# Layer 1 of a two-layer attention kernel: the first query products stand ahead of the last key transposes, the key stores get three buffers at another place, and one weight piece is split sooner

## The chip, the cores and the metric

The kernel runs on one core of a Trainium2 chip. The metric is the time of one execution on the device, in microseconds: 1680.79 us before the change, the median of three runs (1679.54 to 1683.7). A core has five engines that each work off a queue of their own in order and wait for one another through semaphores: TensorE (PE, with its weight loads as PEld), VectorE (DVE), ScalarE (ACT), GpSimd (POOL) and SyncE (SP), which here issues nearly all DMAs.

## The reference

Two layers work on 1024 latent tokens and 256 context tokens of width 1024. Each layer normalizes the rows, scales and shifts them by values computed from a condition vector, and runs an attention mixer whose output is gated, projected and added to the input. Layer 0 is grouped-query attention. Layer 1, where the change lies, is multi-head latent attention:

```
kv_a, k_r, q_a, g = split(h @ w_in, [256, 288, 672])
kv     = rms_norm(kv_a, kv_a_norm) @ w_kv_b          # per head: 64 key and 64 value columns
k_nope = rms_norm(kv[..., :64], k_nope_norm)
k_rope = rope(rms_norm(k_r, k_rope_norm))            # one 32-wide key for all heads
q      = rms_norm(rms_norm(q_a, q_a_norm) @ w_q_b, q_norm)   # 16 heads of 96, the last 32 rotated
p      = softmax((q_nope k_nope + q_rope k_rope) / sqrt(96))  # latent queries, all 1280 keys
y      = (p v * silu(g)) @ w_out
```

Context tokens give keys and values in layer 1, but no queries and no output. All data are 32-bit floats.

## The kernel before

**Precision.** Each product of two fp32 matrices is made of three passes on rounded parts, `hi x hi`, `hi x lo` and `lo x hi` (`mm3`, L90). So each operand is split into a high part, a rounded copy made by ACT, and a low part, the difference, made by DVE or POOL. `load_weight` (L139) does it for weights: a piece of up to 1024 columns is fetched by an SP DMA into one of three raw buffers `wraw`, then `parts` casts it on ACT (L158) and subtracts on DVE or POOL (L137, chosen by a counter and the argument `share`; with `share=1` always DVE). With `todo` given, the pieces are not fetched at once but collected as functions: calling a piece issues its DMA and returns a function that splits it. The split weights lie in a ring of two pairs of buffers.

**Stages of layer 1.** Tokens go in ten tiles of 128, eight latent and two context.

1. `out_proj` of layer 0 makes the new rows; `sink0` normalizes them, and `modulate` turns them to columns and splits them. For the last tile, a context tile, it calls `last0` (L1491), which loads the first weight of layer 1 (`l1_w_in`, columns 0 to 287), adds the last output, multiplies tiles 0 and 1 by that weight (`proj1`, kept in `early`), modulates the context (`flush(1)`), and loads and splits `l1_w_kv_b` (256 x 2048, four pieces).
2. The keys: `staged` (L100) runs stages over the tiles, one tile behind the other. `kv_compress` projects and normalizes (`kvn`, L1529), `kv_latent` transposes and splits the latent, `kv_expand` makes keys (`mmk`) and values (`mmv`) by `l1_w_kv_b`, normalizes the keys (`kn`, L1561) and stores the values, and `kv_store` (L1591) transposes the keys on TensorE (L1597), splits them into `th` (ACT, L1601) and `tl` (DVE, L1602), and stores these with two SP DMAs.
3. The queries: `q_compress` (L1714) multiplies by columns 288 to 671 of `l1_w_in` (`wqa`), squares and sums on ACT (L1718), takes the reciprocal root on POOL (`qa_rs`), scales on DVE (`qan`); `q_latent` transposes and splits that; `q_expand` and `q_store` follow. A second pass makes the other heads. The gate's products are mixed in.
4. Attention over 16 heads, then the output projection.

**Order of the work.** Instructions are placed on the engines' queues by a planner that simulates the program by its own costs: on each engine it takes, among those that are ready, the one that comes first in the program. Inside `tc.manual_schedule(engines=...)`, and `in_order(engine)`, the named engines keep the written order of that block; others may still be put in between. Before the change only DVE is kept in order in the key stage, and nothing in the query stage.

**Memory.** Buffers are taken from pools. The pools of one stage lie on a stack (`side="right"`), and the pools of the next stage lie in the same memory; with `reuse_waits="tile"` a new tile waits for the readers and writers of those old tiles that it overlaps, the DMAs that store them among them. In the key stage the stack holds `wk1b` (six working tiles), `stg1a` (two buffers each of `th`, `tl` and the values `v1`), `latp1a` (four of each latent part) and small tiles. In the query stage `wk1c` (eight working tiles, `sq` and `qan` among them), `stg1b`, `latp1b`, `wqp` (a split weight) and small tiles lie there. Product results lie in PSUM: four buffers `mm` and four `tp` for transposes.

Of the kernel before, what the change touches and what calls it, by code (L numbers as in the profile page):

```python
# [11 lines left out]
F32R = mybir.dt.float32r  # L12
# [7 lines left out]
P = 128  # L20
D = 1024
KT = D // P
# [4 lines left out]
TT = NT // P  # L27
# [5 lines left out]
def raw(ap):  # L33
    return ap.bitcast(F32)
# [3 lines left out]
def hybrid_kernel(ctx: ExitStack, tc: tile.TileContext, ins: dict, out: bass.AP):  # L38
# [12 lines left out]
    def pad(pool, size):  # L51

        pool.tile([P, size // 4], F32, name="pad", tag="pad", bufs=1)
# [28 lines left out]
    def in_order(engine):  # L82

        return tc.manual_schedule(engines={engine})
# [15 lines left out]
    def staged(items, *stages):  # L100

        items = list(items)
        held = {}
        for t in range(len(items) + len(stages) - 1):
            for j, stage in enumerate(stages):
                i = t - j
                if 0 <= i < len(items):
                    held[i] = stage(items[i], held.get(i))
# [17 lines left out]
    def ring_pair(dtype=F32R):  # L126
        a = ring.tile([P, 4096], dtype, name="wa", tag="wa")
        b = ring.tile([P, 4096], dtype, name="wb", tag="wb")
        return a, b
# [3 lines left out]
    def sub_any(lo, a, b, share):  # L133

        lo_turn[0] += 1
        eng = dve if share and lo_turn[0] % share == 0 else pool
        eng.tensor_sub(lo, a, b)  # L137

    def load_weight(w, kt, c0, cols, share=2, slot=None, todo=None):  # L139
        a, b = slot or ring_pair()  # L140
        pitch = -(-cols // 64) * 64
        wh, wl = (t[:, : kt * pitch].rearrange("p (k n) -> p k n", n=pitch)[:, :, :cols] for t in (a, b))
        src = w[:, c0:c0 + cols].rearrange("(k p) n -> p k n", p=P)
        wid = min(cols, 1024)
        step = max(1, 1024 // cols)
        for k in range(0, kt, step):
            for c in range(0, cols, wid):
                n = min(step, kt - k)

                def piece(k=k, n=n, c=c):  # L150
                    r = rawp.tile([P, 1024], F32, name="wraw", tag="wraw")
                    rv = r[:, : n * wid].rearrange("p (k n) -> p k n", n=wid)
                    ks, cs = slice(k, k + n), slice(c, c + wid)
                    sp.dma_start(rv, src[:, ks, cs])

                    def parts(share=share):
                        for j in range(n):
                            act.copy(wh[:, k + j, cs], rv[:, j, :])  # L158
                            sub_any(wl[:, k + j, cs], rv[:, j, :], raw(wh[:, k + j, cs]), share)

                    return parts

                if todo is None:
                    piece()()
                else:
                    todo.append(piece)
        return wh, wl
# [114 lines left out]
    def h_cols(hT, tt):  # L282

        hh, hl = hT[0 if tt < TL else 1]
        cs = slice((tt % TL) * P, (tt % TL + 1) * P)
        return (lambda k: hh[:, k, cs]), (lambda k: hl[:, k, cs])
# [572 lines left out]
    right = dict(side="right", reuse_waits="tile")  # L859
# [7 lines left out]
    small = stR.enter_context(tc.tile_pool(name="sml0", bufs=3, **right))  # L867
    wk = stR.enter_context(tc.tile_pool(name="wk0", bufs=6, **right))
    tab = stR.enter_context(tc.tile_pool(name="tab0", bufs=1, **right))
    sg2 = []  # L870
# [262 lines left out]
    parts = [[ModPart(0, sec, q, 256, lambda: mp[0], 4, wk, ps_mod, ps_tp) for q in range(4)] for sec in range(2)]  # L1133
# [279 lines left out]
    w_in1 = ins["l1_w_in"]  # L1413
    hT1 = []

    def proj1(tt, w, cols):
        ps = ps_mm.tile([P, 512], F32, name="mm", tag="mm")
        lh, ll = h_cols(hT1, tt)
        mm3(ps[:, :cols], lh, ll, lambda k: w[0][:, k, :], lambda k: w[1][:, k, :], range(KT))
        return ps  # L1420
# [32 lines left out]
    with ExitStack() as st:  # L1453
        xp = st.enter_context(tc.tile_pool(name="xpp0", bufs=4, **right))
        gp = st.enter_context(tc.tile_pool(name="gp0", bufs=1, **right))
        wk = st.enter_context(tc.tile_pool(name="wk1a", bufs=3, **right))
        small = st.enter_context(tc.tile_pool(name="sml1a", bufs=3, **right))
        pad(small, 224)
        stO = ExitStack()
        op = stO.enter_context(tc.tile_pool(name="opp0", bufs=3, **right))  # L1460
        hold = []

        def flush(upto):
            while len(hold) >= upto and hold:
                pair, xs = hold.pop(0)
                modulate(1, pair, xs, hT1, ps_tp, wk)

        xs_of = {}

        def sink0(tt, xt):  # L1470
            if tt < TL:
                sp.dma_start(x1d[tt * P:(tt + 1) * P, :], xt)
            norm_rows(xt, small)
            xs_of.setdefault(tt // 2, []).append(xt)
            if tt % 2 == 0:
                flush(1)
            else:
                hold.append((tt // 2, xs_of[tt // 2]))

        def started0():  # L1480
            at.flush()
            stL.close()
            hT1.append(alloc_hT(stl, "hlat1", NL))

        def resid0(tt):
            return x_in[tt * P:(tt + 1) * P, :] if tt < TL else ctx_in[(tt - TL) * P:(tt - TL + 1) * P, :]

        kv_w = []
        early = {}

        def last0(add):  # L1491
            kv_w.append(load_weight(ins["l1_w_in"], KT, 0, 288))
            with tc.manual_schedule(engines={mybir.EngineType.PE, mybir.EngineType.DVE, mybir.EngineType.Activation}):
                add()
                for tt in range(2):
                    early[tt] = proj1(tt, kv_w[0], 288)
                stO.close()
                hT1.append(alloc_hT(stc, "hctx1", NC))
                flush(1)
                kv_w.append(load_weight(ins["l1_w_kv_b"], 2, 0, 2048, 1))  # L1500

        out_proj(0, wo, resid0, sink0, TT, op, xp, gp, ps_mm, first, started0, False, last0)
    hT = hT1

# [2 lines left out]

    with ExitStack() as st:
        wk = st.enter_context(tc.tile_pool(name="wk1b", bufs=6, **right))
        sg2 = st.enter_context(tc.tile_pool(name="stg1a", bufs=2, **right))  # L1510
        latp = st.enter_context(tc.tile_pool(name="latp1a", bufs=4, **right))
        small = st.enter_context(tc.tile_pool(name="sml1b", bufs=3, **right))

        wkvr, wkvb = kv_w
# [76 lines left out]
        def kv_store(tt, held):  # L1591
            cs = slice(tt * P, (tt + 1) * P)
            for g2 in range(2):
                kn = held[g2]
                tp = ps_tp.tile([P, 512], F32, name="tp", tag="tp")
                for j in range(4):
                    pe.transpose(tp[:, j * P:(j + 1) * P], kn[:, j * P:(j + 1) * P], ident)  # L1597
                th = sg2.tile([P, 4, P], F32R, name="th", tag="th")
                tl = sg2.tile([P, 4, P], F32R, name="tl", tag="tl")
                tv = tp.rearrange("p (a n) -> p a n", n=P)  # L1600
                act.activation(th, tv, AF.Copy, scale=w_kn)  # L1601
                dve.scalar_tensor_tensor(tl, tv, w_kn, raw(th), op0=ALU.mult, op1=ALU.subtract)  # L1602
                sp.dma_start(k1h[4 * g2:4 * g2 + 4, :, cs].rearrange("a p n -> p a n"), raw(th))
                sp.dma_start(k1l[4 * g2:4 * g2 + 4, :, cs].rearrange("a p n -> p a n"), raw(tl))

        with in_order(mybir.EngineType.DVE):
            staged(range(TT), kv_compress, kv_latent, later, later, kv_expand, kv_store)
    stK.close()
    stc.close()

# [82 lines left out]
    with ExitStack() as st:  # L1693
        wk = st.enter_context(tc.tile_pool(name="wk1c", bufs=8, **right))
        sg2 = st.enter_context(tc.tile_pool(name="stg1b", bufs=2, **right))
        latp = st.enter_context(tc.tile_pool(name="latp1b", bufs=3, **right))
        wqp = st.enter_context(tc.tile_pool(name="wqp", bufs=1, **right))
        small = st.enter_context(tc.tile_pool(name="sml1c", bufs=3, **right))

        tab = st.enter_context(tc.tile_pool(name="tab1c", bufs=1, **right))  # L1700
        cwq = tab.tile([P, TL, 96], F32, name="cwq")
# [7 lines left out]
                pool.tensor_mul(swq[:, :, o_:o_ + 8], sinB[:, :, o_:o_ + 8],  # L1709
                                w_q[:, 64 + i_:64 + i_ + 8].unsqueeze(1).broadcast_to([P, TL, 8]))  # L1710

        wqa = load_weight(w_in1, KT, 288, 384)

        def q_compress(tt, _):  # L1714
            ps = proj1(tt, wqa, 384)
            ss = small.tile([P, 1], F32, name="qass", tag="qass")
            sq = wk.tile([P, 512], F32, name="sq", tag="w512")
            act.activation(sq[:, :384], ps[:, :384], AF.Square, accum_out=ss)  # L1718
            rs = rstd_of(small, ss, 384, "qa")
            qn = wk.tile([P, 512], F32, name="qan", tag="w512")  # L1720
            dve.scalar_tensor_tensor(qn[:, :384], ps[:, :384], rs, w_qa, op0=ALU.mult, op1=ALU.mult)
            return qn
# [169 lines left out]
```

## Time and profile before

| | |
|---|---|
| median of three runs | 1680.79 us |
| the profiled execution, its own time | 1686.67 us |
| its span, first to last instruction | 1684.9 us |
| mean granted TensorE clock | 0.996 |
| TensorE busy | 1648.9 us |
| VectorE, ScalarE, GpSimd busy | 1046.5, 640.7, 950.6 us |

The profile gives for each engine the busy time in any stretch of the span, and for each instruction its start, its length and what ended the idle time before it. The granted clock is the share of full speed at which TensorE ran. Layer 1's projections begin near 855 us, its key stage fills 855 to 967 us, and the query stage follows up to about 1115 us. Times below are microseconds from the span's start.

### The profile page before, as it was taken

How to read it: one execution, taken by the hardware profiler on the slowest of the kernel's cores; microseconds unless marked ns; L12 is line 12 of the kernel's file. 1: busy time of each engine (PE TensorE's matmuls, PEld its weight loads, DVE VectorE, ACT ScalarE, POOL GpSimd, SP SyncE). 2: the span in 40 equal slices, each digit the busy share in tenths (PEclk: the TensorE clock that was granted, in tenths of full speed). 3: DMA queues.
4: the chain of work that ended last, by engine and by line, in shares of the span. 5: the costliest groups of instructions: out<-in, count | busy, mean ns of one | idle time of the engine just before them, and what ended most of it. 6: DMA issues, size and time to landing. Idle time of an engine off the chain costs nothing. (4 is left out here: it accounts for less than half of the span.)

```text
span 1684.9 us, 27275 instructions
## 1 busy us (share of the span) xinstructions
PE 1648.9 (98%) x10236; PEld 1194.2 (71%) x10236; DVE 1046.5 (62%) x1660; ACT 640.7 (38%) x944; POOL 950.6 (56%) x624
## 2 busy tenths in 40 slices
PE   7999999999999999999989999999999999999998
PEld 5776768875555555468878798886766767767587
DVE  3774553457788877526575657744777777677231
ACT  3642222225454554433244633330534434334310
POOL 2673441118899898833245645450668778777521
PEclk9999999999999999999999999999999999999999
DMA  8548856532352422256324857776566555653451
GB/s 290 194 126 254 253 163 197 156 91 58 83 138 77 126 74 72 79 156 186 125 81 137 241 166 195 222 207 150 127 139 141 133 131 120 133 134 81 121 172 70
DMA packets 221116, 244.21 MB, mean 145 GB/s; under 512 B 23160, under 2 KB 160616, under 8 KB 220984
## 3 DMA queue, kind: packets, MB, share of 16 engines
q1 hardware_dynamic: 220560, 242.36, 51.7%
q8 instruction: 81, 1.33, 0.4%
q14 instruction: 51, 0.42, 0.1%
q10 hardware_dynamic: 424, 0.11, 0.0%
HBM read 168.62 MB, written 73.63 MB: 144 GB/s over the span
## 5 line engine op out<-in xcount | busy, mean ns | idle before, releaser
L552 ACT ACTIVATE p<-st 128x1024 f32<-128x1024 f32 x328 | 335.9, 1027 | 156.9 <-PE st L545 143.2
L586 POOL TENSOR_TENSOR acp<-acp,p 128x1024 f32<-128x1024 f32 x128 | 305.2, 2384 | 8.3 <-ACT p L552 0.4
L394 DVE TENSOR_REDUCE m<-mx 128x1 f32<-128x512 f32 x256 | 176.2, 691 | 94.0 <-PE mx L392 88.1
L430 DVE TENSOR_REDUCE m<-mx 128x1 f32<-128x1024 f32 x128 | 150.4, 1220 | 68.9 <-PE mx L421 68.4
L586 POOL TENSOR_TENSOR acp<-p 128x1024 f32<-128x1024 f32 x34 | 81.5, 2399 | 185.5 <-ACT p L552 185.3
L602 PE MATMUL avt<-p,v 128*64 128x512 f32 x672 | 152.6, 598 | 0.6 <-DVE crow L461 0.3
L586 POOL TENSOR_TENSOR acp<-acp,acd 128x1024 f32<-128x1024 f32 x60 | 142.0, 2366 | 14.6 <-DVE acd L572 11.2
L572 DVE TENSOR_REDUCE acd<-p 128x512 f32<-128x1024 f32 x124 | 144.7, 1220 | 6.9 <-ACT p L552 6.9
L602 PE MATMUL av<-p,v 128*64 128x512 f32 x640 | 141.1, 595 | 0.0
L137 POOL TENSOR_TENSOR wb<-wraw,wa 128x512 fp32r<-128x512 f32 (+3 forms) x65 | 88.4, 1374 | 82.2 <-ACT wa L158 82.2
L94 PE MATMUL mm<-wa,hh 128*128 128x512 f32 (+2 forms) x336 | 127.6, 380 | 1.1 <-ACT hh L959 1.1
L96 PE MATMUL mm<-wa,hl 128*128 128x512 f32 (+2 forms) x336 | 122.0, 363 | 1.5 <-DVE hl L962 1.5
L545 PE MATMUL st<-QH,KH 64*128 64x512 f32 x320 | 122.2, 407 | 0.6 <-DVE gth L304 0.5
L95 PE MATMUL mm<-wb,hh 128*128 128x512 f32 (+2 forms) x336 | 121.3, 361 | 0.0
L545 PE MATMUL st<-QH,KL 64*128 64x512 f32 x320 | 117.7, 391 | 0.0
L545 PE MATMUL st<-QL,KH 64*128 64x512 f32 x320 | 117.2, 390 | 0.0
L94 PE MATMUL y<-wa,oh 128*128 128x512 f32 (+1 forms) x296 | 114.1, 385 | 0.6 <-ACT oh L798 0.6
L95 PE MATMUL y<-wb,oh 128*128 128x512 f32 (+1 forms) x296 | 113.5, 384 | 0.0
L96 PE MATMUL y<-wa,ol 128*128 128x512 f32 (+1 forms) x296 | 113.5, 384 | 0.0
L602 PEld LDWEIGHTS av<-p,v 128*64 128x64 f32 x640 | 44.4, 137 | 88.3 <-issue 87.6
L602 PEld LDWEIGHTS avt<-p,v 128*64 128x64 f32 x672 | 44.9, 136 | 86.9 <-issue 80.6
L94 PE MATMUL mm<-hh,wa 128*128 128x512 f32 (+1 forms) x264 | 103.2, 391 | 0.1
(247 smaller groups left out, 4039.2 us busy)
## 6 DMA issues: line engine op xcount, KB each, us to landing
mraw<-in_l_w_mod SPq DMA_DIRECT2D x64, 256.0 KB
wraw<-in_l_w_in SPq DMA_DIRECT2D x28, 512.0 KB
KH<-k1h SPq DMA_DIRECT2D x32, 320.0 KB
KL<-k1l SPq DMA_DIRECT2D x32, 320.0 KB
rb<-rrow SPq DMA_DIRECT2D x72, 128.0 KB
mraw<-in_l_w_mod SPq DMA_DIRECT2D x16, 512.0 KB
QA<-q0h SPq DMA_DIRECT2D x32, 256.0 KB
wraw<-in_l_w_out SPq DMA_DIRECT2D x16, 512.0 KB
```

The costliest lines, as they stand in the source:

```text
L94: pe.matmul(ps, lhsT=lh(k), rhs=rh(k), start=first and i == 0, stop=False)
L95: pe.matmul(ps, lhsT=lh(k), rhs=rl(k), start=False, stop=False)
L96: pe.matmul(ps, lhsT=ll(k), rhs=rh(k), start=False, stop=last and i == len(ks) - 1)
L137: eng.tensor_sub(lo, a, b)
L394: dve.reduce_max(s["m"][:, i, n:n + 1], held["m"], axis=AX.X)
L430: dve.reduce_max(s["m"][:, i, 0:1], m, axis=AX.X)
L545: pe.matmul(ps[:, n * 512:(n + 1) * 512], lhsT=lh, rhs=rh, start=j == 0, stop=j == last)
L552: act.activation(p, ps, AF.Exp, scale=self.ops["scale"])
L572: dve.reduce_sum(t[:, ns], p2.rearrange("p a n -> p n a")[:, ns, :], axis=AX.X)
L586: pool.tensor_add(t, a, b)
L602: pe.matmul(s["av"][64 * n:64 * n + 64, :], lhsT=s["v"][:, kt, u["vc"]:u["vc"] + 64], rhs=p[:, n * 512:(n + 1) * 512], start=kt == kts[0], ...
```

## The change

- In `last0`, `l1_w_kv_b` is taken in pieces: the DMAs of the first three are called ahead of `add()`; the first piece is split, and the fourth fetched, right behind the two early products and ahead of the context modulation; the other three pieces are split where all four were.
- `kv_store` of the last tile is taken out of the key stage. `wqa` is loaded directly behind that stage, and a block with written order on PE and DVE holds the first query tile's 24 products, then the last tile's `kv_store`. `q_compress` takes the first tile's result from `early`.
- `th` and `tl` have three buffers. The pool of the latents, `latp1a`, lies ahead of `stg1a` on the stack, and in the query stage the small tiles lie ahead of `wqp`.

```diff
         def last0(add):
             kv_w.append(load_weight(ins["l1_w_in"], KT, 0, 288))
             with tc.manual_schedule(engines={mybir.EngineType.PE, mybir.EngineType.DVE, mybir.EngineType.Activation}):
+                todo = []
+                kv_w.append(load_weight(ins["l1_w_kv_b"], 2, 0, 2048, 1, todo=todo))
+                parts = [piece() for piece in todo[:3]]
                 add()
                 for tt in range(2):
                     early[tt] = proj1(tt, kv_w[0], 288)
+                parts[0]()
+                parts.append(todo[3]())
                 stO.close()
                 hT1.append(alloc_hT(stc, "hctx1", NC))
                 flush(1)
-                kv_w.append(load_weight(ins["l1_w_kv_b"], 2, 0, 2048, 1))
+                for part in parts[1:]:
+                    part()
...
         wk = st.enter_context(tc.tile_pool(name="wk1b", bufs=6, **right))
+        latp = st.enter_context(tc.tile_pool(name="latp1a", bufs=4, **right))
         sg2 = st.enter_context(tc.tile_pool(name="stg1a", bufs=2, **right))
-        latp = st.enter_context(tc.tile_pool(name="latp1a", bufs=4, **right))
...
-                th = sg2.tile([P, 4, P], F32R, name="th", tag="th")
-                tl = sg2.tile([P, 4, P], F32R, name="tl", tag="tl")
+                th = sg2.tile([P, 4, P], F32R, name="th", tag="th", bufs=3)
+                tl = sg2.tile([P, 4, P], F32R, name="tl", tag="tl", bufs=3)
...
+        kept = []
+
+        def store_all_but_last(tt, held):
+            kept.append(held) if tt == TT - 1 else kv_store(tt, held)
+
         with in_order(mybir.EngineType.DVE):
-            staged(range(TT), kv_compress, kv_latent, later, later, kv_expand, kv_store)
+            staged(range(TT), kv_compress, kv_latent, later, later, kv_expand, store_all_but_last)
+        wqa = load_weight(w_in1, KT, 288, 384)
+        with tc.manual_schedule(engines={mybir.EngineType.PE, mybir.EngineType.DVE}):
+            early[0] = proj1(0, wqa, 384)
+            kv_store(TT - 1, kept[0])
...
+        small = st.enter_context(tc.tile_pool(name="sml1c", bufs=3, **right))
         wqp = st.enter_context(tc.tile_pool(name="wqp", bufs=1, **right))
-        small = st.enter_context(tc.tile_pool(name="sml1c", bufs=3, **right))
...
-        wqa = load_weight(w_in1, KT, 288, 384)
-
         def q_compress(tt, _):
-            ps = proj1(tt, wqa, 384)
+            ps = early.pop(tt, None) or proj1(tt, wqa, 384)
```

## The prediction

> **What bounds the kernel now.** I read the page first, then the busy time by stretches, then TensorE's instructions in order of time with their waits, and last the chain of waits.
>
> ```profile
> span 1684.9 us, 27275 instructions
> PE 1648.9 (98%) x10236; PEld 1194.2 (71%) x10236; DVE 1046.5 (62%) x1660; ACT 640.7 (38%) x944; POOL 950.6 (56%) x624
> ```
>
> TensorE is busy for all but 36.0 of 1684.9 us, so the change can only earn what TensorE idles, or runs slowly, in the two places that it touches. The stretches show these places (columns: stretch; busy of PE, weight loads, DVE, ACT, POOL; granted clock; DMA share; GB/s):
>
> ```profile
> 860.00:890.00 30.00, 25.42 (x154) 22.14 (x153) 19.80 (x55) 13.24 (x40) 11.21 (x21) 0.89 0.30 95
> ...
> 960.00:990.00 30.00, 25.15 (x140) 23.83 (x140) 15.74 (x27) 14.64 (x30) 15.78 (x12) 0.94 0.86 258
> 990.00:1010.00 20.00, 20.00 (x119) 19.93 (x118) 13.44 (x41) 4.85 (x12) 8.40 (x13) 1.00 0.24 71
> ...
> 880.00:885.00 5.00, 5.00 (x15) 3.71 (x16) 2.08 (x10) 1.99 (x9) 2.75 (x10) 0.50 0.23 77
> 980.00:985.00 5.00, 4.58 (x20) 4.51 (x21) 3.40 (x7) 4.14 (x10) 4.02 (x3) 0.66 0.54 165
> ```
>
> Idle are 30 - 25.42 = 4.6 us at the start of the layer 1 keys and 30 - 25.15 = 4.9 us where keys hand over to queries. Behind them none is idle in 20: a microsecond won at either place is passed on. At both the clock falls (0.50, 0.66), behind these waits (columns: start, length, engine, line, operation, and in brackets the idle time before it and its releaser):
>
> ```profile
> 876.59 0.40 PE L96 MATMUL mmk<-wa,kvl 128*128 128x512 f32 x1
> 879.96 0.66 PE L1548 MATMUL tp<-ident,kvn 128*128 128x128 f32 x2 [2.97 <-DVE kvn L1529]
> 880.27 0.78 PE L94 MATMUL mmv<-wa,kvh 128*128 128x512 f32 x1
> ...
> 886.15 0.39 PE L94 MATMUL mmv<-wa,kvh 128*128 128x512 f32 x1
> ...
> 887.51 0.29 PE L94 MATMUL mm<-wa,hh 128*128 128x288 f32 x1
> ...
> 962.34 1.03 PE L1597 MATMUL tp<-ident,kn 128*128 128x128 f32 x8
> 965.34 0.63 PE L1597 MATMUL tp<-ident,kn 128*128 128x128 f32 x4 [1.97 <-DVE kn L1561]
> ...
> 966.94 0.63 PE L1597 MATMUL tp<-ident,kn 128*128 128x128 f32 x4 [0.80 <-DVE kn L1561]
> 967.33 0.42 PE L95 MATMUL mm<-wb,hh 128*128 128x384 f32 x1
> ...
> 978.01 0.34 PE L96 MATMUL mm<-wa,hl 128*128 128x384 f32 x1
> 980.42 0.52 PE L1728 MATMUL tp<-ident,qan 128*128 128x128 f32 x3 [2.08 <-DVE qa_ms L118]
> ...
> 981.30 0.41 PE L94 MATMUL mm<-wa,hh 128*128 128x384 f32 x1
> ...
> 984.72 0.39 PE L94 MATMUL mm<-wa,hh 128*128 128x384 f32 x1
> ```
>
> The slow clock has a price beside the idle time. Between 880.27 and 886.15 stand 12 key and value products and 4 small transposes in 5.88 us; the six products from 886.15 to 887.51 took 1.36, so at full clock this were 2.72 + about 0.35 = 3.1: 2.8 us lost. Between 967.33 and 978.01 are 61 query products at 0.175 us; from 981.30 to 984.72 nine products and three transposes took 3.42, at full clock 1.58 + 0.27: 1.6 us lost. So the first place holds 2.97 + 2.8 = 5.8 us, the second 1.97 + 0.80 + 2.08 + 1.6 = 6.4 us.
>
> **Part one, the expansion weight.** Its four pieces pass through three raw buffers, so the fourth is fetched only when the first has been split:
>
> ```profile
> 854.98 17.32 SPq L154 DMA_DIRECT2D wraw<-in_l_w_kv_b  x4
> ...
> 875.90 1.05 ACT L158 CAST wa<-wraw 128x1024 fp32r<-128x1024 f32 x1 [3.07 <-DMA wraw<-in_l_w_kv_b]
> ...
> 861.85 1.90 DVE L275 TENSOR_SCALAR hmod<-tp,A,B 128x256 f32<-128x256 f32 x4 [1.28 <-PE tp L271]
> ...
> 870.72 3.49 DVE L137 TENSOR_TENSOR wb<-wraw,wa 128x1024 fp32r<-128x1024 f32 x3
> ...
> 875.31 0.42 DVE L88 TENSOR_TENSOR kvl<-tp,kvh 128x256 fp32r<-128x256 f32 x1
> 876.99 1.22 DVE L137 TENSOR_TENSOR wb<-wraw,wa 128x1024 fp32r<-128x1024 f32 x1 [1.26 <-ACT wa L158]
> 878.13 0.27 DVE L88 TENSOR_TENSOR krl<-tp,krh 32x128 fp32r<-32x128 f32 x1
> 879.33 0.48 DVE L1529 SCALAR_TENSOR_TENSOR kvn<-mm,kvrs,bc_l_kv_a_norm 128x256 f32<-128x256 f32 x1 [0.81 <-POOL kvrs L1527]
> 879.89 0.42 DVE L88 TENSOR_TENSOR kvl<-tp,kvh 128x256 fp32r<-128x256 f32 x1
> 880.62 0.28 DVE L88 TENSOR_TENSOR krl<-tp,krh 32x128 fp32r<-32x128 f32 x1 [0.32 <-ACT krh L87]
> ...
> 881.84 0.48 DVE L1529 SCALAR_TENSOR_TENSOR kvn<-mm,kvrs,bc_l_kv_a_norm 128x256 f32<-128x256 f32 x1 [0.82 <-POOL kvrs L1527]
> ```
>
> VectorE's queue holds the subtraction for the fourth piece ahead of `krl` and of the third tile's `kvn`, for which TensorE waits 2.97 us. After the change one cast (1.05 us or a little less) and one subtraction (1.22) move ahead of the context modulation. VectorE has a hole of 1.28 us ahead of its first `hmod`, into which 1.22 fits; without that cover the modulation slips by at most 1.22, and TensorE has products to do then. The fourth DMA leaves near 862, not 872.3 (854.98 + 17.32), and has landed long before the three remaining pieces are split, in the 3.49 us where three are split now. SP is set free as early; the three other DMAs that move pass no store, as the last output tile is a context tile. The four context low parts swap engines (the counter that alternates DVE and POOL is one further); that I cost at nothing, plus or minus 0.7 us, half a piece's subtraction.
>
> Then `krl` follows `kvl` as it does one tile later, 880.62 - 879.89 = 0.73: at 876.04 in place of 878.13. All behind it is 2.09 us earlier: `kvn` at 877.24, the transposes at 877.87, a wait of 0.9 us behind 876.99. What is late next is the same chain for the fourth tile: from `kvn` to `kvn` it takes 881.84 - 879.33 = 2.51 us, against about 1.7 us of full-clock work, so another 0.8 us, and its small rope part perhaps 0.5. Started at 877.87, with 18 products (880.27 to 887.51) in 3 x 1.36 = 4.1 us, transposes in about 0.6 and these 1.3, the next tile's projection starts near 883.9 instead of 887.51: 3.6 us. I take 3.0, as the planner sets TensorE's order here and won't place each transpose where it fits. Ends: 2.1, if the clock falls nevertheless, and 5.8, if no wait is left.
>
> **Part two, the first query products ahead of the last transposes.** The weight for them was split long before:
>
> ```profile
> 942.49 0.55 DVE L137 TENSOR_TENSOR wb<-wraw,wa 128x384 fp32r<-128x384 f32 x1
> ...
> 960.49 0.59 ACT L1583 COPY v<-mmv 128x512 f32<-128x512 f32 x1 [0.26 <-DMA vd<-v]
> ...
> 964.50 0.69 DVE L1561 TENSOR_TENSOR kn<-mmk,kn_rs 128x512 f32<-128x512 f32 x1 [1.02 <-POOL kn_rs L120]
> ```
>
> So 24 products of 0.175 = 4.2 us stand from 963.1 to 967.3, and the last eight transposes follow at 967.3; their inputs are there at 965.2 and 966.8. Both waits are covered: 2.8 us won. The lower end: the products need one of four PSUM buffers. One comes free with the value copy at 961.1, the next key buffer only at 965.2; were it that one, 2.1 us of the 2.8 would be lost: 0.7.
>
> **Part three, three key buffers and other places.** The query wait of 2.08 us hangs on this piece of the chain:
>
> ```profile
> 967.94 4.23 DMA k1h<-th
> 972.27 0.70 ACT th L1601
> ...
> 973.77 4.20 DMA k1l<-tl
> 978.23 0.59 ACT sq L1718 x2
> 979.07 0.56 POOL qa_rs L120
> ```
>
> The last `th` waits for a store to leave its buffer, and the first `sq` waits for the store of the last `tl`, although it reads nothing of it: the new tile lies where the old one was. With three buffers the first wait goes; with the latents moved between, `sq` lies on latents, whose products ended by 962.3. Behind the products' end at 967.3 `sq` to transposes takes 980.42 - 978.23 = 2.2 us, so about 969.8, if POOL is free. It isn't:
>
> ```profile
> 967.02 4.35 POOL L137 TENSOR_TENSOR wqb<-wraw,wqa 128x768 fp32r<-128x768 f32 x2 [0.94 <-ACT wqa L158]
> ```
>
> If both these splits stay ahead of `qa_rs`, it starts at 971.4 and the transposes at 971.4 + (980.42 - 979.07) = 972.7. TensorE has its transposes to 968.1 and the second tile's products to 972.3. I expect a wait of 0.6 us: of 2.08 + 1.6 = 3.7 the change keeps 3.0, say 2.7 for the new ties (the query latents now lie on the last `th` and `tl`, and ACT's next `sq` is queued behind the one that waits for those stores). Ends: 3.7, and -2.5, if the planner sets the transposes right behind 968.1 (4.6 us and a slow stretch of 1.6).
>
> **The sum.** 3.0 + 2.8 + 2.7 = 8.5 us. The profiled execution took 1686.7 us with a span of 1684.9, the runs' median is 1680.8; idle time and slow clock are absolute, so I take 8.5 from both: 1678.2 profiled, 1672.3 for the median.
>
> The Trainium skill (TensorE: Matmul & The Clock Gate, Part 1) says that the clock halves after at least one idle window of some 3.4 us. Here 2.08 us of idle were enough, with 0.66 granted in the stretch behind, so the measurement decides; taken at its word the rule would say that the gaps are not the cause.
>
> **The rivals.**
> - *The waits move.* TensorE's next inputs come late in both places, and the clock still falls. For it: the fourth tile's chain of 2.51 us and POOL's 4.35 us. Against it: the new waits, 0.9 and 0.6 us, are shorter than 1.97, behind which the products ran on at 0.175. Then 2.1 + 2.8 and a third place at nought: 4.9 at best, with a longer query wait some 3.5; 1677.
> - *The first products don't start early,* for want of a PSUM buffer: 8.5 - 2.1 = 6.4; 1674.4. For it: only one product stood between the two halves of the last transposes. Against it: the copy at 960.49.
> - *The clock falls for a reason other than the gaps.* The slow stretches stay: 2.1 us is left of the 3.0 at the first place, and 2.7 - 1.6 = 1.1 at the third part, with 2.8 between them 6.0; 1674.8. Against it: both stretches directly follow the longest waits.
> - *Slower.* Outside hand-written blocks the planner orders TensorE by its own times. Without the long wait at the start it may set each query tile's transposes too close behind its products, for all eight tiles. The chain from `sq` on is 2.2 us; it decides once fewer than 2.2 / 0.175 = 13 products lie between. At 1.6 us for each tile that is 13 us: 1672.3 + 13 = 1685. Against it: none of the seven later tiles waits now (990 to 1010 is full).
>
> **How the numbers follow.** Forecast 0.58, waits move 0.20, no early start 0.09, clock of its own 0.05, slower 0.08. What a measurement of this kernel tells from no change is about 0.3%, 5.0 us: from 1675.8 to 1685.8. The forecast's own range is 1669 to 1676. Faster: 0.56 of the forecast, 0.06 of no early start, 0.03 of the clock case: 0.65. Slower 0.05, as half of its case lies beyond 1685.8; the rest, 0.30, is within. The range goes from 1667.5 (all 5.8 + 6.4 = 12.2 us won is 1668.6, and the runs lie up to 1.2 below their median) to 1680.5, which leaves out the slower case and little else.
>
> **What would show it.** Right: no DMA wait of ACT at the fourth weight piece, a wait below 1.2 us at the third tile's transposes with clock 1.00 behind it, 24 products of 384 columns straight behind 962 and no `kn` wait, `sq` without a `k1l` wait, clock 1.00 behind the first query transposes. Wrong: a query wait of 2 us on POOL or a store, a clock of 0.5 in either place, or new waits at later query transposes.

## Result: a gain half as large as forecast

The median of 8 runs is 1677.1 us after the change (1676.46 to 1682.35), against 1683.08 of 8 runs of the kernel before beside it. The ratio is 0.9975 (0.9964 to 0.9986), so about 4.2 us are won. It leaves out one run of before that took 1823.73 us, far longer than all others; the medians of the remaining runs lie 5.7 us apart. The same file timed again on another occasion gave 1676.32 against 1681.11, ratio 0.9968 (0.9957 to 0.9979), 5.4 us. Forecast were 8.5 us.

The profiled execution has a span of 1674.9 us, 10 less than the one of before. That difference flatters the change, since the profiled execution of before, at 1686.7 us, was one of its longest. Of the 10 us, 3.0 had arisen before layer 1 began, where nothing was changed. The stretches of the changed kernel (columns as in the prediction):

```profile
860.00:890.00 30.00, 25.03 (x152) 20.90 (x152) 18.79 (x58) 14.12 (x47) 13.09 (x25) 1.00 0.25 78
960.00:990.00 30.00, 30.00 (x182) 29.83 (x181) 19.81 (x39) 13.92 (x31) 17.72 (x16) 1.00 0.84 247
...
1010.00:1030.00 20.00, 18.22 (x106) 16.91 (x105) 16.19 (x46) 7.95 (x18) 10.46 (x13) 1.00 0.77 222
```

At the start of the keys TensorE still idles 5.0 us of 30. At the handover it idles not at all, and its clock is 1.00 in both. So the second place went as planned and the first did not. TensorE's rows at the two places (start, length, engine, line, operation, and in brackets the idle time and its releaser):

```profile
858.19 1.91 PE L271 MATMUL tp<-ident,xt 128*128 128x128 f32 x16
...
865.37 0.44 PE L1554 MATMUL tp<-ident,kvn 128*128 128x128 f32 x2 [1.31 <-DVE kvn L1535]
...
870.17 0.41 PE L1554 MATMUL tp<-ident,kvn 128*128 128x128 f32 x2 [1.22 <-DVE kvn L1535]
...
873.74 0.47 PE L94 MATMUL mmk<-wa,kvh 128*128 128x512 f32 x1 [0.65 <-DVE kvn L1536]
...
876.98 0.41 PE L1554 MATMUL tp<-ident,kvn 128*128 128x128 f32 x2 [1.19 <-DVE kvn L1535]
...
957.79 1.03 PE L1603 MATMUL tp<-ident,kn 128*128 128x128 f32 x8
962.85 1.03 PE L1603 MATMUL tp<-ident,kn 128*128 128x128 f32 x8
972.74 0.49 PE L1741 MATMUL tp<-ident,qan 128*128 128x128 f32 x3
```

In the lower half all waits of 1.97, 0.80 and 2.08 us are gone. In the upper half the wait of 2.97 us for the third tile's `kvn` became one of 1.19, but these transposes still stand 876.98 - 858.19 = 18.8 us behind the last context transposes. Before, it was 879.96 - 861.21 = 18.75. These are the rows of before ahead of the third tile:

```profile
861.21 1.91 PE L271 MATMUL tp<-ident,xt 128*128 128x128 f32 x16
...
866.16 0.44 PE L1548 MATMUL tp<-ident,kvn 128*128 128x128 f32 x2 [1.19 <-DVE kvn L1529]
...
870.14 0.28 PE L1549 MATMUL tp<-ident,kvn 128*32 128x128 f32 x1 [0.38 <-DVE kvn L1541]
```

Up to there TensorE waited 1.19 + 0.38 = 1.6 us before and 1.31 + 1.22 + 0.65 = 3.2 after. So what was won at the third tile (2.97 - 1.19 = 1.8) had been lost at the first two.

### The profile page after: what moved, and what is told of

It is laid out like the page before. It is cut to its first block, busy times and chain, and to the rows that moved or that the text cites. A ratio compares the mean times of both kernels' runs of the same rounds, so it can differ in the third digit from the quotient of the medians.

```text
span 1674.9 us, 27270 instructions
## 1 busy us (share of the span) xinstructions
PE 1643.2 (98%) x10236; PEld 1189.1 (71%) x10236; DVE 1046.0 (62%) x1660; ACT 640.3 (38%) x944; POOL 949.0 (57%) x624
## 3 DMA queue, kind: packets, MB, share of 16 engines
q8 instruction: 81, 1.33, 0.3%
## 4 chain that ended last, share of the span: by engine, by line
PE 83%; DVE 6%; POOL 4%; issue 3%; DMA 2%; ACT 1%; SPq 0%; ACTq 0%; DVEq 0%; POOLq 0%
PE st L545 19%; PE avt L602 8%; PE av L602 8%; PE mm L94 7%; PE mm L96 7%; PE mm L95 7%; PE mx L392 4%; PE y L94 3%; PE y L95 3%; PE y L96 3%; PE mx L421 2%; PE mx L647 1%; PE pm L201 1%; DVE wb L137 1%; PE mx L402 1%
```

## Experiments

A gain is the ratio's distance from 1 times the median of before in the same comparison (1681.1 to 1682.2 us); the medians' own differences lie within 1.1 us of it.

**The changed kernel again, the two halves apart, and the engines' turns.** The first run is the changed file, unaltered. The next two each make one half of the change: only the weight piece in `last0`, or only the handover with its buffers and places. The fourth is the whole change with the context low parts on the engines that they had before:

```
                 parts[0]()
+                lo_turn[0] -= 1
                 parts.append(todo[3]())
                 ...
                 flush(1)
+                lo_turn[0] += 1
```

> The changed kernel as it is, to see how executions spread. Between the two profiled executions the span fell by 9.95 us, of which 3.0 us were won before layer 1 began, where nothing was changed. Theory 1 (the waits and their slow clock are always there): the change is worth about 7 us in every pair, ratio 0.9958. Theory 2 (the slow clock behind a wait comes in some executions only): 4 to 5 us on the mean, ratio 0.997 to 0.9975, and executions with a lower mean clock are the longer ones, by half of the time at half clock.

> Only the weight piece is split sooner; keys and queries as before. The forecast's sum says 3.0 us of gain at the first place (16.4 us from the context's transposes to the third tile's, in place of 18.75). The theory from the traces: 18.8 us as in the changed kernel, since the third tile's transposes are held by the same queue on VectorE, and about 1.5 us to the next projection if the clock stays full; timed 0 to 2 us.

> Only the handover is changed; the weight piece as before. Forecast: 5.5 us at the second place. From the traces: 6.9 us between the eighth tile's key transposes and the fourth query tile's, where slow clock had 1.6 of it, and some 1.4 us given back in the second query pass; timed 4 to 5.5 us. If instead the gain hangs on both parts together, this kernel alone gains less than 3.

> The changed kernel, with the counter that alternates DVE and POOL taken one back ahead of the context modulation and put right behind it, so that the four context low parts are on the engines that they had before the change. Theory: in the changed kernel the fourth low part sits on POOL ahead of the second tile's reciprocal root (867.55 to 868.85), VectorE waits 1.81 us for it with three weight subtractions queued behind, and this eats the 2.09 us that the early piece should win. Then here the third tile's transposes follow the context's first ones after 16.5 to 17 us in place of 18.8, and the span is 1.5 to 2.1 us shorter than the changed kernel's. Rival: the chain of the tiles on VectorE sets the pace whatever the engines; then 18.8 stays.

Measured: the changed kernel again 1676.32. The weight piece alone 1680.82, ratio 0.9999 (0.999 to 1.0008): nothing. The handover alone 1677.19, 0.9974 (0.9966 to 0.9983): 4.4 us, all of the gain. The whole with the old turns 1675.3, 0.9963 (0.9951 to 0.9976): 6.2 us. The 0.9968 of the changed kernel lies between the two theories about the slow clock (0.9958 and 0.997) and decides neither. The halves came out as expected from the traces. With the old turns the third tile's transposes stand 16.92 us behind the context's, as expected, but the time is only 1.0 us below the changed kernel's, not 1.5 to 2.1; and the step that counts turned out to be another than the second tile's reciprocal root, as the next rows show.

**The weight piece with the old turns.** The same two lines in the kernel that has only the first half.

> Part one alone, but the four context low parts stay on the engines that they had before. Theory: the swap of engines, costed at nothing in the forecast, made the first tile's latent transposes 2.23 us later and ate what part one won; without it they stand 4.9 us behind the last context transposes (7.18 with the swap), the third tile's near 16.5 us (18.75 before), and the time is 1.9 us below that of part one with the swap, about 1679. Rival: the place had little to win, since the 6.8 us of half clock in the profile of before are not in most runs; then the transposes come sooner, and the time is still within 1 us of the kernel before (1681).

Measured: 1678.75, ratio 0.9986 (0.9977 to 0.9995), a gain of 2.35 us where the same half without the two lines had none. That is the theory's figure, not the rival's. GpSimd's queue shows why; first the changed kernel, then this one with TensorE's rows:

```profile
862.85 1.29 POOL L137 TENSOR_TENSOR hl<-hmod,hh 128x512 fp32r<-128x512 f32 x1 [6.08 <-ACT hh L279]
864.09 0.70 POOL L1533 TENSOR_TENSOR kvrs<-kvms,mhalf 128x2 f32<-128x2 f32 x1
```

```profile
859.26 1.29 POOL L137 TENSOR_TENSOR hl<-hmod,hh 128x512 fp32r<-128x512 f32 x1 [3.78 <-ACT hh L279]
860.51 0.71 POOL L1535 TENSOR_TENSOR kvrs<-kvms,mhalf 128x2 f32<-128x2 f32 x1
```

```profile
856.90 1.91 PE L271 MATMUL tp<-ident,xt 128*128 128x128 f32 x16
...
861.79 0.44 PE L1556 MATMUL tp<-ident,kvn 128*128 128x128 f32 x2 [1.13 <-DVE kvn L1537]
...
873.86 0.41 PE L1556 MATMUL tp<-ident,kvn 128*128 128x128 f32 x2 [1.23 <-DVE kvn L1537]
```

GpSimd holds the first tile's `kvrs` behind its first context part. With the old turns that is the part that is ready first, 859.26 - 856.90 = 2.36 us behind the context transposes. With the turns swapped it is the next one, 862.85 - 858.19 = 4.66 us behind. So `kvrs`, `kvn` and the first transposes come 2.3 us later (7.18 us behind the context transposes in place of 4.89). VectorE, which keeps the written order, carries the delay on to the third tile. First the changed kernel, then the one with the old turns:

```profile
864.83 0.48 DVE L1535 SCALAR_TENSOR_TENSOR kvn<-mm,kvrs,bc_l_kv_a_norm 128x256 f32<-128x256 f32 x1 [1.70 <-POOL kvrs L1533]
...
869.94 3.49 DVE L137 TENSOR_TENSOR wb<-wraw,wa 128x1024 fp32r<-128x1024 f32 x3
```

```profile
861.25 0.48 DVE L1537 SCALAR_TENSOR_TENSOR kvn<-mm,kvrs,bc_l_kv_a_norm 128x256 f32<-128x256 f32 x1 [1.33 <-POOL kvrs L1535]
...
866.36 3.49 DVE L137 TENSOR_TENSOR wb<-wraw,wa 128x1024 fp32r<-128x1024 f32 x3
```

From the first `kvn` to the three splits it takes 5.11 us in both, so nothing more is lost between them. The pairs of kernels differ by about as much: the halves alone by 2.2 us (2.35 and 0.17), the whole by 1.0 us of time, and by 1.9 us in the trace up to the first key transposes (33.8 and 31.9 us from the last context transposes).

**A second profile of before.**

> The kernel before once more, for a second profile of it. The forecast took the slow clock of both places (2.8 and 1.6 us) as part of every execution. If so, the granted clock is about 0.5 again behind the 2.97 us wait for the third tile's normalised keys and about 0.66 behind the 2.08 us query wait, and from the last context transposes to the ninth tile's key transposes it takes 101 us as in the first profile. Rival: the waits come each time but the slow clock only in some executions; then the waits of 2.97, 1.97, 0.80 and 2.08 us are all there, and a stretch whose clock stayed at 1.00 is shorter by 1.7 us for each 3.4 us of half clock that is missing: 97.7 to 99.4 us.

It took 1681.59 us (span 1679.8). The waits came again (those for the last keys with 1.82 and 0.80 us), the query wait shorter, and half as much half clock came at the first place, none at the second:

```profile
877.79 0.53 PE L1548 MATMUL tp<-ident,kvn 128*128 128x128 f32 x2 [3.02 <-DVE kvn L1529]
...
976.91 0.52 PE L1728 MATMUL tp<-ident,qan 128*128 128x128 f32 x3 [1.31 <-DVE qa_ms L118]
```

```profile
870.00:890.00 20.00, 16.95 (x91) 13.97 (x90) 11.96 (x37) 8.35 (x31) 8.45 (x19) 0.91 0.38 118
...
970.00:990.00 20.00, 18.69 (x112) 18.32 (x111) 11.35 (x27) 8.90 (x22) 10.27 (x11) 1.00 0.88 260
```

From the last context transposes to the ninth tile's key transposes it took 100.75 us, 0.38 less than in the first profile, although 3.4 us less of it ran at half clock; 1.7 us was the rival's figure. The theory that the slow clock belongs to every execution falls, and the rival's price of it is too high as well.

**Each half of the handover alone.** One kernel has only the early products, with two key buffers and the pools where they were. The other has only three buffers and the new places. A third is the whole change, with the old turns, and two key buffers:

```
-                th = sg2.tile([P, 4, P], F32R, name="th", tag="th", bufs=3)
-                tl = sg2.tile([P, 4, P], F32R, name="tl", tag="tl", bufs=3)
+                th = sg2.tile([P, 4, P], F32R, name="th", tag="th")
+                tl = sg2.tile([P, 4, P], F32R, name="tl", tag="tl")
```

> Only the first query tile's 24 products stand ahead of the last eight key transposes; key stores in two buffers and all pools where they were. If parts two and three add up as in the forecast, the waits of 1.97 and 0.80 us for the normalised keys are gone, the query wait of about 2 us stays, and the time falls by 2.8 us (1678.3). Rival: the two need each other, the wait is only moved on to the query transposes, which still hang on the stores of the last keys; then the time falls by less than 1 us.

> Only the three key buffers and the pools' new places; the first query tile's products stand behind the last transposes, as before. If parts two and three add up as in the forecast, the query wait (2.08, 1.31 us in two profiles of before) shrinks to 0.6 or less, the 1.97 and 0.80 us for the normalised keys stay, and the time falls by 2.7 us (1678.6). Rival: with the last stores out of the way the wait was the price of the order alone, and the parts are one thing, of which this half is worth 4 us or more, since the first half alone made the kernel slower.

> The changed kernel with the low parts' engines as before, but the key parts in two buffers again; pools in their new places. If the third buffer is needed, the last key parts on ScalarE wait for a store (2.7 us in the kernel with early products alone), the first query squares are queued behind them, and TensorE waits 1 to 3 us for the first query transposes: 1677 to 1679. If the places alone do it, the squares wait for no store and the time stays at 1675.

Measured: early products alone 1686.08, ratio 1.0035 (1.0023 to 1.0047), slower by some 5.9 us. Places and buffers alone 1681.41, 0.9993 (0.9984 to 1.0002), no difference. Two buffers 1679.07, 0.9987 (0.9977 to 0.9997), so 4 us of the 6.2 are lost without the third buffer. Of these expectations the additive ones failed for both halves: +5.9 and -1.2 do not add to -4.4. The early products' rival had the wait rightly moved on to the query transposes, but had not expected a loss. For places alone the rival's 4 us or more failed too. For two buffers the expectation held, though the wait came out longer than its 1 to 3 us. In the kernel with early products alone, TensorE's and ScalarE's rows, and the stretch behind the wait, are:

```profile
979.97 0.87 PE L1735 MATMUL tp<-ident,qan 128*128 128x128 f32 x3 [5.22 <-DVE qa_ms L118]
```

```profile
969.39 0.69 ACT L1601 ACTIVATE th<-tp,w_kn 128x512 fp32r<-128x512 f32 x1 [2.68 <-DMA k1h<-th]
...
977.77 0.49 ACT L1725 ACTIVATE sq<-mm 128x384 f32<-128x384 f32 x1 [2.00 <-DMA k1l<-tl]
```

```profile
980.00:985.00 5.00, 5.00 (x21) 4.90 (x22) 3.77 (x6) 2.46 (x7) 3.58 (x4) 0.60 0.45 121
```

The query chain is tied to the key stores, not to TensorE's products: `sq` waits for the last `tl` to leave, as before. Work taken ahead of the wait only makes the wait longer, here 5.22 us, and the clock drops behind it (0.60). That explains why nothing is won, and not the whole loss: from the last context transposes to the first query parts' transposes this profile takes 152.2 us, the two of before 153.5 and 150.7. Where the rest of the 5.9 us arises is not shown; the mean granted clock of these six runs was 0.9955, against 0.9973 before. With two buffers in the new places `sq` waits for no store, but the `th` ahead of it on ScalarE does:

```profile
964.18 0.69 ACT L1609 ACTIVATE th<-tp,w_kn 128x512 fp32r<-128x512 f32 x1 [2.63 <-DMA k1h<-th]
```

```profile
973.08 0.52 PE L1743 MATMUL tp<-ident,qan 128*128 128x128 f32 x3 [3.50 <-DVE qa_ms L118]
```

So TensorE waits 3.50 us at the query transposes. With places and buffers alone no query wait is left; the waits for `kn` stay, and in the profiled execution 3.4 us of half clock stood behind them (TensorE's row at the first of the two, then the stretch):

```profile
961.23 0.63 PE L1597 MATMUL tp<-ident,kn 128*128 128x128 f32 x4 [1.90 <-DVE kn L1561]
```

```profile
962.00:973.00 11.00, 10.20 (x52) 10.20 (x52) 5.65 (x8) 4.04 (x7) 4.22 (x3) 0.84 0.87 241
```

**The give-back at the second query pass.** In the changed kernel one TensorE wait became longer, at the end of the first query pass; it is idle 20 - 18.22 = 1.8 us in the stretch from 1010 to 1030. First before, then after, both counted from the first query parts' transposes:

```profile
1014.75 0.82 PE L1778 MATMUL tp<-ident,t 128*128 128x128 f32 x6
...
1028.55 0.52 PE L1778 MATMUL tp<-ident,t 128*128 128x128 f32 x3 [0.87 <-DVE tl L88]
...
1046.79 0.82 PE L1778 MATMUL tp<-ident,t 128*128 128x128 f32 x6
```

```profile
1003.29 0.82 PE L1791 MATMUL tp<-ident,t 128*128 128x128 f32 x6
...
1018.02 0.52 PE L1791 MATMUL tp<-ident,t 128*128 128x128 f32 x3 [1.78 <-DVE tl L88]
...
1036.27 0.82 PE L1791 MATMUL tp<-ident,t 128*128 128x128 f32 x6
```

From the first row to the last it takes 32.0 us before and 33.0 after. TensorE is 1014.75 - 1003.29 = 11.5 us ahead of before at the first row. VectorE is only 10.1 us ahead at the third query tile's `qal` (990.65 before, 980.54 after), and 9.4 and 10.0 at the next two; splits of the gate's weight stand ahead of it. First before, then after:

```profile
990.65 0.55 DVE L88 TENSOR_TENSOR qal<-tp,qah 128x384 fp32r<-128x384 f32 x1
```

```profile
979.28 1.33 DVE L137 TENSOR_TENSOR wb<-wraw,wa 128x512 fp32r<-128x512 f32 x1
980.54 0.54 DVE L88 TENSOR_TENSOR qal<-tp,qah 128x384 fp32r<-128x384 f32 x1
```

Two kernels, both with the whole change and the old turns, test that. One puts all eight subtractions on VectorE, the other spreads them over the third to sixth query tile:

```
-        wg = load_weight(w_in1, KT, 672, 512)
+        wg = load_weight(w_in1, KT, 672, 512, 1)
```

```
-        wg = load_weight(w_in1, KT, 672, 512)
+        wg_todo = []
+        wg = load_weight(w_in1, KT, 672, 512, todo=wg_todo)
+        wg_parts = [piece() for piece in wg_todo[:3]]
...
+        def split_late(tt, held):
+            if 2 <= tt <= 5:
+                wg_parts.pop(0)()
+                if tt == 2:
+                    wg_parts.append(wg_todo[3]())
+            return held
...
-        staged(range(TL), q_compress, q_latent, later, expand(0), ...
+        staged(range(TL), q_compress, q_latent, split_late, expand(0), ...
```

> The changed kernel with the context low parts' engines as before, and all eight subtractions for the gate's weight on VectorE, none on GpSimd. Theory: the 1.4 us that the changed kernel gives back between the eighth tile's latent transposes and the second query pass come from these splits, which stood on both engines while TensorE waited before, and now stand ahead of the third query tile's work; VectorE runs 1.35 us behind TensorE's gain from there on. Without GpSimd's half (1.3 to 1.7 us each) less is queued ahead of it: the second pass's first transposes come 32.1 us behind the first pass's (33.0 in the changed kernel, 32.0 before), and the time is 1 us below 1675.3. Rival: the loss is made at the second pass's own weight, whose subtraction takes 1.58 us there; then it stays 33.0 and the time stays.

> The changed kernel with the low parts' engines as before, and the splits of the gate's weight spread over the third to sixth query tile, instead of standing in one row ahead of the third tile's work. Theory: the row makes VectorE late by 1.35 us, which costs 0.95 us at the second query pass; with all eight subtractions on VectorE half of that was gone. Spread out, the second pass's first transposes come 32.0 us behind the first pass's (33.0 in the changed kernel, 32.65 with VectorE alone), and the time is 0.9 us below 1675, about 1674.3, no more than a measurement can just tell. Rival: each split delays the tile in which it stands just as much; then it stays at 33.0 and 1675.

Measured: on VectorE alone 1674.71, ratio 0.9963 (0.9951 to 0.9975); spread 1676.0, 0.9958 (0.9945 to 0.9972). Neither time differs from the 0.9963 without the edit. In the trace the distance is 32.65 and 33.05 us. So the first removed a third of the 0.95 us and the second none. Spread out, VectorE's `qal` for the fourth tile stands 4.5 us behind that tile's transposes, as in the changed kernel (4.4; 2.3 before). With all eight on VectorE it is 2.3 again, and two thirds of the loss are left all the same. Where they arise, the rows of the second pass's own weight show, the place that the first expectation's rival had named. Before, after, and with the gate's splits on VectorE alone:

```profile
1022.30 0.95 DVE L137 TENSOR_TENSOR wb<-wraw,wa 128x768 fp32r<-128x768 f32 x1
...
1023.74 1.22 DVE L118 TENSOR_SCALAR q_ms<-qss 128x4 f32<-128x4 f32 x1
...
1022.29 2.65 POOL L137 TENSOR_TENSOR wb<-wraw,wa 128x768 fp32r<-128x768 f32 x1 [1.03 <-ACT wa L158]
```

```profile
1012.19 1.58 DVE L137 TENSOR_TENSOR wb<-wraw,wa 128x768 fp32r<-128x768 f32 x1
...
1014.27 0.17 DVE L118 TENSOR_SCALAR q_ms<-qss 128x4 f32<-128x4 f32 x1
...
1011.12 1.84 POOL L137 TENSOR_TENSOR wb<-wraw,wa 128x768 fp32r<-128x768 f32 x1
```

```profile
1010.12 2.45 DVE L137 TENSOR_TENSOR wb<-wraw,wa 128x768 fp32r<-128x768 f32 x1
...
1009.93 1.83 POOL L137 TENSOR_TENSOR wb<-wraw,wa 128x768 fp32r<-128x768 f32 x1 [0.84 <-ACT wa L158]
```

Before, both engines begin within 0.02 us of each other and VectorE's subtraction takes 0.95. After, VectorE comes 1.07 us behind GpSimd and needs 1.58; with the gate's splits on VectorE it comes only 0.19 behind, and needs 2.45. Counted from the first query parts' transposes, the `q_ms` that follows ends 0.94 and 0.62 us later than before (in the third kernel it starts at 1013.07, and those transposes at 1002.41), and the distance of 32.0 us grew by 0.94 and 0.61. All thirteen profiles agree: in the six where the two begin within 0.02 us the distance is 32.0 to 32.1, and in the seven where GpSimd is 0.19 us or more ahead it is 32.65 to 33.05. The six are those in which a key store held back ScalarE's last `th` or first `sq` by 2 us or more; that VectorE had time for the splits there, while the query chain stood still, is argued and not shown. No run changes the order at this weight alone.

**What the slow clock costs.** 60 runs of the kernel before, from the three comparisons, lie between 0.995 and 0.999 of mean granted clock, on average 0.9973: (1 - 0.9973) x 1681 = 4.5 us lost in each on average. Taken within each comparison, a run with 1 us more of lost clock is 0.27 us longer (least squares, standard error 0.10; the clock is given to three places, which draws this down somewhat). The traces show one reason. From the last context transposes to the first key transposes the code is the same in four kernels, and in their five profiles the time was 33.61 us with no half clock, 34.24, 34.40 and 34.57 with 3.4 us of it, and 35.25 with 6.8. So 6.8 us at half clock cost 1.64, not 3.4. TensorE was busy 2.0 us longer (30.67 in place of 28.65) and idle 0.4 less: part of the half clock fell into the wait itself (0.85 granted from 877.0 to 879.9, where no product runs), and at full clock TensorE has two waits of 0.2 for GpSimd's part of `kvn`, which are not there at half clock. The ends of the range, without half clock (early products alone, start and end) and with 6.8 us (before, the end):

```profile
860.84 1.91 PE L271 MATMUL tp<-ident,xt 128*128 128x128 f32 x16
...
894.45 0.38 PE L1597 MATMUL tp<-ident,kn 128*128 128x128 f32 x2
```

```profile
896.46 0.82 PE L1597 MATMUL tp<-ident,kn 128*128 128x128 f32 x6
```

(861.21, the start of before, is shown with the result.) Against the same 33.61 us the first half of the change takes 33.84 as it is and 31.97 with the old turns.

## Why the prediction was wrong

**The step that failed first** is the sentence on the context low parts, "that I cost at nothing, plus or minus 0.7 us". The swap cost about 2 us (2.2 between the two kernels with the first half alone, 1.0 between those with the whole change; in both pairs the gains' intervals overlap, and the traces' 2.3 and 1.9 us agree with them) and took what part one won: 3.0 was forecast and 0.2 measured (-1.3 to 1.7). The bound had been half a piece's duration. The cost was a queue position: the swap decides behind which part GpSimd's `kvrs` stands, and that is one step of the modulation, 2.3 us. The mechanism of part one itself was right. The fourth piece is fetched early (no transfer wait of ScalarE there), `krl` and `kvn` no longer stand behind its split, and with the old turns it earns 2.35 us (0.8 to 3.9). That lies near the lower end of 2.1, though in its profile the clock did not fall. All signs that the prediction had named for being right came true, the wait below 1.2 us at the third tile (1.19) with full clock behind it among them: they looked at the third tile, and the loss stood ahead of it.

**The second failed step** is to take the slow clock of one execution as there in every run. The size was right for that execution. At the first place the sum sets 1.3 us of new waits against the 2.8 us of lost work and has 6.0 us from the third tile's transposes to the next projection (877.87 to 883.9); early products alone, without half clock, took 6.03 (879.45 to 885.48), and before 7.55 (879.96 to 887.51). At the query transposes nine products and three transposes took 3.42 us at half clock and 1.90 in the second profile of before, so 1.5 were lost where 1.6 had been reckoned. But 6.8 us at half clock came in one of five profiles of the first place, and the five cost 0.8 us on average, half of the 1.64 of that one; behind the query wait the clock fell in one of the two profiles of before. By the prediction's own rival, which leaves 6.0 us, the clock carried 8.5 - 6.0 = 2.5 us. Half of that, an estimate from these few profiles, makes the forecast 7.2. The runs say much the same: at 0.27 us for each us of lost clock, the 2.8 and 1.6 are worth 1.2. The execution from which they were read was 5.9 us above the median, and the forecast took the whole from that median too.

**Parts two and three** were forecast at 2.8 + 2.7 = 5.5 us and measured together at 4.4 (2.9 to 5.7). The waits went as described: the products stand right behind 957.79, no `kn` wait, no store wait of `sq`. The query wait is even 0, not 0.6, but that is luck. Both splits of `wqb` did stay ahead of `qa_rs`, as feared, but ScalarE's casts of the same weight now stand ahead of the first `sq` too, and the chain came 3.1 us later than reckoned: `qa_rs` at 969.92, 12.1 us behind the ninth tile's key transposes, where 971.4 - 962.34 = 9.1 had been expected. `qan` ends at 971.1:

```profile
970.50 0.62 DVE L1734 SCALAR_TENSOR_TENSOR qan<-mm,qa_rs,bc_l_q_a_norm 128x384 f32<-128x384 f32 x1 [2.21 <-POOL qa_rs L120]
```

TensorE does not wait for it because 52 products, not the second tile's 24, stand ahead of the first query transposes; behind 24 of them (963.64 + 4.2 = 967.8) the wait would have been some 3 us, an estimate from these rows. Also, the two terms were not separate gains. The 2.8 would have been lost again at the query transposes, as the early products alone show; only buffers and places let the chain follow. And 0.95 us were given back at the second pass, where the order of VectorE and GpSimd at its weight turned round; for this place the prediction had no term.

**The rivals.** *The waits move* came true in part: at the first place (3.2 us at the first two tiles in place of 1.6), for another reason than the fourth tile's chain, and at the second pass. Its clock did not fall and its longer query wait did not come, so that its 1677 is the time measured is luck. *No early start* is refuted by 957.79 and 962.85 with 24 products between. *A clock of its own* is refuted: in the six profiles of the whole handover with its three buffers no half clock stands there, and in five of the seven others it does. *Slower*: none of the later transposes of `qan` waits.

On the clock, the Trainium skill (TensorE: Matmul & The Clock Gate, Part 1) has it halve after at least one idle window of about 3.4 us, and says that this window runs freely, so that the same kernel has more or fewer slow products at its start from run to run. Such a difference was seen here in mid-kernel: one and the same wait of 2.83 to 3.02 us was followed by 0, 3.4, 3.4, 3.4 and 6.8 us at half clock in five executions. These waits are all shorter than the window. The prediction had weighed only the first statement.

## To carry to other kernels

A change that shifts an alternating counter moves every later piece to the other engine; look at which small operation stands behind each piece in that engine's queue, not at the piece's duration. Before idle time in front of a step is filled, follow what releases the step: if it is a transfer that does not come sooner, the wait only grows, and filling and freeing are worth something together that neither is worth alone. Take what a single execution shows of the clock as that execution's, and price it by what the engine would have waited for anyway.

## What was not expected of the hardware

Half clock came in stretches of 3.41 us or twice that, except the one that the end of the kernel cuts off. A wait of 2.08 us was followed by it where another of 1.31 was not, and one and the same pair of waits for the last keys (1.82 to 1.97, then 0.80 us) was followed by it in two of five profiles. Subtractions for the weights on VectorE and GpSimd seem to take turns, whichever began first. GpSimd's row beside VectorE's at 979.28 above, in the changed kernel:

```profile
978.77 1.30 POOL L137 TENSOR_TENSOR wb<-wraw,wa 128x512 fp32r<-128x512 f32 x1
```

Where GpSimd began first (978.77) it took 1.30 us, and VectorE's subtraction, begun at 979.28, took 1.33. Where the two began together, at the second pass's weight before (1022.30 and 1022.29), VectorE's took 0.95 and GpSimd's 2.65, and VectorE's next small operation but one, `q_ms`, took 1.22 us in place of 0.17. With all eight on VectorE they took 0.64 each:

```profile
978.23 1.28 DVE L137 TENSOR_TENSOR wb<-wraw,wa 128x512 fp32r<-128x512 f32 x2
```

The fastest versions are the whole change with the old turns, 6.2 us (4.0 to 8.2) below before, and its two variants, which no run here tells from it. Beside the changed kernel in the same comparison it is 1.0 us ahead (1675.3 and 1676.32), less than a measurement can tell.
